# A two-block kernel's expert layer: 64 tokens' first product by gathered rows, dense product at 320 columns, gathers and one-hots placed anew

## The chip, the core and the metric

The kernel runs on one core of a Trainium2 chip. The time is the device time of one execution in microseconds. The engines are TensorE (PE, matmuls; PEld its weight loads), VectorE (DVE), ScalarE (ACT), GpSimd (POOL) and SyncE (SP, which only issues transfers).

## The reference, cut to what matters

The program is two transformer blocks on 512 tokens of width 1024. The change lies in the last layer of the second block, a layer of 16,384 experts (128 x 128), of which each token uses 8 x 16 = 128. Heads and halves choose the experts, the gates are a softmax over 16 scores, and each chosen expert is one row of `expert_u` and one row of `expert_v`.

```python
q = (xb @ w_query).reshape(T, 8, 2, 128)
s = einsum('thpk,hpnk->thpn', q, sub_keys)
top_s, top_i = top_k(s, 16)
cand_s = top_s[:, :, 0, :, None] + top_s[:, :, 1, None, :]
cand_i = top_i[:, :, 0, :, None] * 128 + top_i[:, :, 1, None, :]
best_s, best_pos = top_k(cand_s.reshape(T, 8, 256), 16)
idx = take_along_axis(cand_i..., best_pos)
gate = softmax(best_s)
act = gelu(einsum('td,thkd->thk', xb, expert_u[idx]))
out = einsum('thk,thkd->td', gate * act, expert_v[idx])
```

## The kernel before, in words

The tokens are four tiles of 128. Tile 0 takes the literal way: for each of its 128 choices a **gather**, an indirect DMA that POOL issues (line L1074), brings one row of u, later of v, per token into one of four row buffers (`grow`), and DVE makes one pass over the 128 x 1024 buffer: a product with the tokens' rows `h2`, summed to one number per token (L1077), or an addition of the v row times its weight to `acc0` (L1079). That makes 256 gathers. They are all in `experts_out`.

Tiles 1 to 3 (384 tokens) take the dense way. For each of 128 units j (128 experts each) the **u product** `expert_in` (L1056) multiplies the unit's u weights with all 384 tokens: a weight of 128 x 1024 is loaded, ACT makes its high part (L201), POOL or DVE the rest by a subtraction (L202), and TensorE runs 8 x 3 matmuls of 384 columns (L207 to L209); a gelu follows (L1062). The result is multiplied with a dense matrix of gates, which is zero where a token did not choose the expert, and the **v product** (18 matmuls of 512 columns a unit) adds into six PSUM banks.

The layer runs in this order. `route` (L1088) makes the **keys** in 16 steps (a query product of 24 matmuls of 512 columns, key scores, and the best 16 of 128 on DVE), and then the **selection** for the four tiles in turn (8 steps each: 2048 sums of candidates, best 16 of 256 for each head, masked products on POOL at L1136 that pick the indices, softmax). The indices `eid` and gates of tile 0 serve the gathers; those of the others are transposed into `sel`. `gates_dense` (L1171) makes the **one-hots** in 12 groups of 32 tokens: for each four tokens, four rows A (a one-hot of i times the gate) and one broadcast compare B (one-hot of j), and 128 x 128 matmuls of the two give the 16,384 gates of a token. A comes from POOL for two of eight fours (`GP`, L1188), from ACT for two (`GA`, L1192, L1193, with the gate then on DVE's B at L1195) and from DVE for four (L1199); B is L1202; ACT copies the result to `gst` (L1206), and it goes to DRAM (`gD`). `experts_out` (L1214) is the **output**: gates come back from `gD`, and unit by unit the gated u results go through the v product.

A pace table in `peer` (L1024) spreads 64 of the 128 u products (the even units) between the steps of `route` and `gates_dense`, with their subtraction on POOL; their results are spilled to DRAM (`actD`) and read back in the output. The other 64 are made in the output, with the subtraction on DVE, beside the 256 gathers (one to three a unit).

What is written here is not the order on the engines: a planner takes the program with its dependencies and buffers, places each instruction at its engine's next free time by its own table of durations, the earlier in the program first, and so fixes one order for each engine and for each DMA queue. On the chip each engine works through its order strictly, so an instruction that waits holds back all behind it on that engine.

```python
pace = [(1, 3), (15, 10), (32, 37), (24, 14)]
...
for steps, us in pace:
    for i in range(steps):
        _advance(work)
        for _ in range((i + 1) * us // steps - i * us // steps):
            act = self.expert_in(self.gpool or Q, psp, 2 * j, nc.gpsimd, ...)
```

## Time and profile before

| | |
|---|---|
| median of 3 runs | 2302.53 us (2298.85 to 2306.55) |
| the profiled execution's own time | 2311.13 us |
| its span in the profile | 2309.4 us |
| mean granted clock of TensorE | 0.983 of full speed |
| busy over the span: PE, DVE, ACT, POOL | 2211.4, 1645.3, 955.0, 841.4 us |
| moved by DMA | 469.53 MB, 203 GB/s over the span |

A row of a group reads: line, engine, operation, tiles written and read with their shapes, count, then busy time in us and the mean length of one in ns, then the idle time of the engine just before them and what ended it. A row of the timeline begins with the start in us from the span's start and the length in us. Instructions of one engine can overlap a little, so that the mean times the count can be more than the busy time.

### The profile page before, as it was taken

The page shows a single profiled execution, that of the slowest core. Times are in us where ns is not written, and L with a number is a line of the kernel's source. Part 1 is how long each engine was busy: PE and PEld are TensorE (multiplying, and loading weights), DVE is VectorE, ACT ScalarE, POOL GpSimd, SP SyncE. Part 2 cuts the span into 40 slices and gives each one's busy share as a digit, 9 for nine tenths or more (in the row PEclk, how much of TensorE's full clock was granted, in tenths as well). Part 3 has the DMA queues.
Part 4 walks back from the last instruction along what each step waited for, and adds up shares of the span by engine and source line. Part 5 has one row for each costly group of instructions (what it writes and reads, how often), then busy time and mean ns, then how long its engine had stood idle before and what let it go on. Part 6 is the DMA issues. An engine that isn't in the chain of part 4 may idle for free. (4 is left out here: it accounts for less than half of the span.)

```text
span 2309.4 us, 32140 instructions
## 1 busy us (share of the span) xinstructions
PE 2211.4 (96%) x11849; PEld 1959.7 (85%) x11849; DVE 1645.3 (71%) x3065; ACT 955.0 (41%) x1540; POOL 841.4 (36%) x619
## 2 busy tenths in 40 slices
PE   7898999999999999999998899979999999999997
PEld 6687888888888888888898889968888888888886
DVE  4336556878635468556589899768888877888888
ACT  4215444343425533353333489823333333333332
POOL 3133210000002224231458898624444444445445
PEclk9998899999999999999999999989999999999999
DMA  7423104766422321053344456799999999899996
GB/s 245 124 63 96 38 1 157 241 216 221 134 100 77 110 76 53 20 185 105 108 145 141 151 189 229 270 326 348 341 341 342 348 347 345 318 336 342 351 333 218
DMA packets 165646, 469.53 MB, mean 203 GB/s; under 512 B 18801, under 2 KB 62705, under 8 KB 165361
## 3 DMA queue, kind: packets, MB, share of 16 engines
q1 hardware_dynamic: 128624, 333.25, 42.3%
q0 software_dynamic: 36864, 134.23, 15.9%
q8 instruction: 93, 1.52, 0.3%
q14 instruction: 65, 0.52, 0.1%
HBM read 422.31 MB, written 39.85 MB: 200 GB/s over the span
## 5 line engine op out<-in xcount | busy, mean ns | idle before, releaser
L207 PE MATMUL b<-hh,wlo 128*128 128x384 f32 (+2 forms) x1872 | 656.1, 352 | 10.7 <-ACT act L1062 5.5
L208 PE MATMUL b<-hl,whi 128*128 128x384 f32 (+2 forms) x1872 | 654.2, 350 | 3.9 <-DVE hl L289 3.3
L209 PE MATMUL b<-hh,whi 128*128 128x384 f32 (+2 forms) x1872 | 653.3, 350 | 0.0
L201 ACT ACTIVATE whi<-raw 128x1024 fp32r<-128x1024 f32 (+1 forms) x405 | 426.3, 1057 | 388.8 <-PE b L209 164.7
L202 DVE TENSOR_TENSOR wlo<-raw,whi 128x1024 fp32r<-128x1024 f32 (+1 forms) x326 | 396.8, 1226 | 216.5 <-ACT whi L201 211.4
L207 PEld LDWEIGHTS b<-hh,wlo 128*128 128x128 f32 x1872 | 354.3, 190 | 38.8 <-issue 7.5
L208 PEld LDWEIGHTS b<-hl,whi 128*128 128x128 f32 x1872 | 355.1, 190 | 31.0 <-DVE hl L289 3.8
L202 POOL TENSOR_TENSOR wlo<-raw,whi 128x1024 fp32r<-128x1024 f32 x79 | 199.6, 2540 | 494.9 <-ACT whi L201 485.6
L209 PEld LDWEIGHTS b<-hh,whi 128*128 128x128 f32 x1872 | 354.7, 189 | 25.3 <-issue 0.4
L207 PE MATMUL b<-whi,wl 128*128 128x512 f32 x768 | 299.9, 390 | 13.1 <-DVE wl L1250 13.1
L208 PE MATMUL b<-wlo,wh 128*128 128x512 f32 x768 | 300.8, 392 | 0.0
L209 PE MATMUL b<-whi,wh 128*128 128x512 f32 x768 | 300.7, 392 | 0.0
L1074 POOL DMA_INDIRECT grow<-in_p_ur_dram,eid x128 | 170.7, 1334 | 249.7 <-DVE gact L1077 173.1
L1074 POOL DMA_INDIRECT grow<-in_p_v_dram,eid x128 | 175.3, 1370 | 208.4 <-DVE acc L1079 131.2
L1062 ACT ACTIVATE act<-b 128x384 f32<-128x384 f32 x114 | 55.8, 491 | 351.3 <-PE b L209 315.3
L207 PE MATMUL b<-whi,hl 128*128 128x512 f32 (+1 forms) x464 | 181.0, 391 | 4.4 <-DVE hl L255 2.4
L207 PEld LDWEIGHTS b<-whi,wl 128*128 128x128 f32 x768 | 144.8, 189 | 42.3 <-DVE wl L1250 13.5
L209 PE MATMUL b<-whi,hh 128*128 128x512 f32 (+1 forms) x464 | 179.6, 387 | 0.0
L208 PE MATMUL b<-wlo,hh 128*128 128x512 f32 (+1 forms) x464 | 179.6, 387 | 0.0
L209 PEld LDWEIGHTS b<-whi,wh 128*128 128x128 f32 x768 | 144.7, 188 | 30.3
L208 PEld LDWEIGHTS b<-wlo,wh 128*128 128x128 f32 x768 | 144.7, 188 | 29.0
L1079 DVE SCALAR_TENSOR_TENSOR acc<-grow,gact,acc 128x1024 f32<-128x1024 f32 x127 | 162.5, 1280 | 6.9 <-DMA grow<-in_p_v_dram,eid 5.7
(296 smaller groups left out, 3065.5 us busy)
## 6 DMA issues: line engine op xcount, KB each, us to landing
raw<-in_p_u_dram SPq DMA_DIRECT2D x128, 512.0 KB, 4.4
raw<-in_p_v_dram SPq DMA_DIRECT2D x128, 512.0 KB, 6.7
raw<-in_w_adaT_dram SPq DMA_DIRECT2D x48, 512.0 KB, 4.2
gD<-gst SPq DMA_DIRECT2D x48, 512.0 KB, 4.3
gt<-gD SPq DMA_DIRECT2D x16, 1536.0 KB, 13.0
raw<-in_w_up_dram SPq DMA_DIRECT2D x44, 512.0 KB, 4.2
raw<-in_w_t_dram SPq DMA_DIRECT2D x32, 512.0 KB, 3.6
acts<-actD SPq DMA_DIRECT2D x64, 192.0 KB, 5.7
```

Source lines behind the costliest of these rows:

```text
L201: nc.scalar.activation(hi, raw, AF.Copy)
L202: (eng or nc.vector).tensor_tensor(lo, raw, hi.bitcast(F32), op=ALU.subtract)
L207: mm(out, al, bh, start=start, stop=False)
L208: mm(out, ah, bl, start=False, stop=False)
L209: mm(out, ah, bh, start=False, stop=stop)
L1062: self.nc.scalar.activation(act, ps, AF.Gelu)
L1074: nc.gpsimd.indirect_dma_start(out=g, out_offset=None, in_=rows[n], in_offset=bass.IndirectOffsetOnAxis(ap=self.eid[:, s:s + 1], axis=0))
L1079: nc.vector.scalar_tensor_tensor(self.acc0, g, act[:, s:s + 1], self.acc0, op0=ALU.mult, op1=ALU.add)
```

## The change

64 of tile 1's tokens leave the dense u product. Tokens 0 to 63 of tile 1 have their 128 choices gathered as 64 gathers of 128 rows (64 tokens, two choices at a time: the upper half of the partitions holds choices 64 to 127, with copies of the indices `eid1` and of the tokens' rows `h2b`). DVE makes one pass over each, and the gelu of the 128 numbers times the gate takes the gate's place in `sel`, so that the activation comes in with the gates; the u results of these 64 tokens are set to 1.0 in the output. Their v product stays dense. The dense u product has 320 columns.

96 of the 128 u products are now made before the output and 32 (every fourth unit) in it. The selection's order is tile 1, 0, 2, 3. The gathers of tile 1 are spread over the selection from tile 0's steps on; 22 of tile 0's gathers lie in the selection, 48 in the one-hots and 187 steps in the output. POOL makes the rows A for four of eight fours instead of two, ACT for two (both steps on ACT, the gate included), DVE for two; for the two groups of 32 tokens that hold tile 1's 64, ACT's two go to DVE, and these groups come last. In the one-hots the u products' subtraction is on DVE instead of POOL. The one-hot matmuls write PSUM with a stride of four elements, and ACT's copy writes runs of four. The pool of split weights is opened anew for the second mixer (8 buffers) and for this layer (6 instead of 8).

```diff
-NSPILL = 64
+NSPILL = 96
+NIN = 320
...
-GP, GA = (2, 6), (0, 4)
+GP, GA = (0, 2, 4, 6), (1, 5)
...
+NACT = 6
...
             if n == 2:
+                wsp.close()
                 late = ctx.enter_context(tc.tile_pool(name="late", bufs=1, reuse_waits="tile"))
                 self.h2 = late.tile([128, D], F32, name="h2")
+            if n > 1:
+                wsp.close()
+                wsp = ctx.enter_context(ExitStack())
+                self.wsp = wsp.enter_context(tc.tile_pool(name=f"wsp{n}", bufs=8 if n == 2 else 6, reuse_waits="tile"))
...
-                                rows=None if tt else self.h2)
+                                rows={0: self.h2, 1: self.h2b}.get(tt))
+            nc.sync.dma_start(self.h2b[64:128], self.h2b[0:64])
...
-                pace = [(1, 3), (15, 10), (32, 37), (24, 14)]
...
+                pace = [(1, 3, 0, 0), (15, 12, 0, 0), (8, 10, 0, 0), (8, 14, 24, 0), (16, 29, 40, 22), (24, 28, 0, 48)]
+                self.pend = []
+                work = [self.route(Q, psp, sel, iota), self.gates_dense(psp, sel, iota)]
+                g1 = [self.gather1(Q, psp, sel)]
+                todo, self.gpool = list(self.slot), None
+                for steps, cols, r1, r0 in pace:
                     for i in range(steps):
+                        part = lambda k: (i + 1) * k // steps - i * k // steps
                         _advance(work)
...
+                        for _ in range(part(cols)):
+                            act = (self.gpool or Q).tile([128, NIN], F32, name="act", bufs=4)
+                            j = todo.pop(0)
+                            self.expert_in(act, psp, j, nc.vector if self.gpool else nc.gpsimd)
+                            nc.sync.dma_start(self.actD[self.slot[j]], act)
+                        _advance(g1, part(r1))
+                        _advance(g0, part(r0))
...
+        ps = psp.tile([128, S], F32, name="u")[:, :NIN]
+        self.proj_t(ps, w, self.hh, self.hl, slice(S - NIN, S))
         self.nc.scalar.activation(act, ps, AF.Gelu)
...
+    def row(self, n, eid):
+        g = self.grows.tile([128, D], F32, name="grow")
+        self.nc.gpsimd.indirect_dma_start(out=g, out_offset=None, in_=self.a[n].rearrange("j i d -> (j i) d"),
+                                          in_offset=bass.IndirectOffsetOnAxis(ap=eid, axis=0))
+        return g
...
+    def gather1(self, Q, psp, sel):
+
+        nc = self.nc
+        act = Q.tile([128, 64], F32, name="gact1")
+        for k in range(64):
+            g = self.row("p_ur", self.eid1[:, k:k + 1])
+            nc.vector.tensor_tensor_reduce(g, g, self.h2b, 1.0, 0.0, ALU.mult, ALU.add, act[:, k:k + 1])
+            if k < 63:
+                yield
+        both = Q.tile([64, 128], F32, name="gact2")
+        nc.scalar.activation(act, act, AF.Gelu)
+        nc.sync.dma_start(both[:, 0:64], act[0:64])
+        nc.sync.dma_start(both[:, 64:128], act[64:128])
+        nc.vector.tensor_tensor(both, both, self.gate1, op=ALU.mult)
+        ps = psp.tile([128, NT, 128], F32, name="t")
+        nc.tensor.transpose(ps[:, 0, :64], both, self.ident[:64, :64])
+        nc.scalar.activation(sel[2][:, 0, :64], ps[:, 0, :64], AF.Copy)
...
-            for t in range(NT):
+            for t in (1, 0, 2, 3):
...
-            for c in range(12):
+            for c in list(range(2, 12)) + [0, 1]:
...
-                    if t4 in GP:
-                        for i in range(4):
-                            nc.gpsimd.tensor_scalar(A[:, i], iota, ii[:, i:i + 1], gg[:, i:i + 1], op0=ALU.is_equal,
-                                                    op1=ALU.mult)
-                    elif t4 in GA:
+                    if t4 in GA and c > 1:
+
                         for i in range(4):
                             nc.scalar.activation(A[:, i], iota, AF.Abs, bias=ii[:, i:i + 1], scale=-1.0)
-                        nc.scalar.activation(A, A, AF.Relu, bias=self.ones, scale=-1.0)
                         for i in range(4):
-                            nc.vector.tensor_scalar(B[:, i], iota, jj[:, i:i + 1], gg[:, i:i + 1], op0=ALU.is_equal,
-                                                    op1=ALU.mult)
+                            nc.scalar.activation(A[:, i], A[:, i], AF.Relu, bias=gg[:, i:i + 1], scale=ng[:, i:i + 1])
                     else:
+                        eng = nc.gpsimd if t4 in GP else nc.vector
                         for i in range(4):
...
+                            eng.tensor_scalar(A[:, i], iota, ii[:, i:i + 1], gg[:, i:i + 1], op0=ALU.is_equal,
+                                              op1=ALU.mult)
...
                     for i in range(4):
-                        nc.tensor.matmul(ps[:, i, :], A[:, i, :], B[:, i, :], start=True, stop=True)
-                    nc.scalar.activation(st.rearrange("p j t -> p t j")[:, 4 * t4:4 * t4 + 4, :], ps, AF.Copy)
+                        nc.tensor.matmul(ps.rearrange("p (j t) -> p t j", t=4)[:, i, :], A[:, i, :], B[:, i, :],
+                                         start=True, stop=True)
+                    nc.scalar.activation(st[:, :, 4 * t4:4 * t4 + 4], ps.rearrange("p (j t) -> p j t", t=4), AF.Copy)
...
+            acts = [P.tile([128, n], F32, name=f"acts{i}") for i in range(NACT)]
+            for t in acts:
+                nc.gpsimd.memset(t[:, :n - NIN], 1.0)
```

## Rows read from the trace of the kernel before

**Rows 1.** Busy time of each engine by stretch; the first line names the columns.

```profile
core 0: us, PE busy (x) PEld busy (x) DVE busy (x) ACT busy (x) POOL busy (x), PEclk, DMA share, GB/s
989.00:1173.00 184.00, 179.73 (x948) 162.91 (x949) 99.71 (x505) 67.42 (x98) 56.26 (x26) 0.99 0.40 133
1173.00:1337.00 164.00, 148.28 (x837) 146.58 (x837) 153.58 (x352) 62.75 (x88) 126.21 (x42) 0.96 0.49 148
1337.00:1490.00 153.00, 146.44 (x1107) 144.31 (x1106) 142.56 (x367) 147.94 (x246) 127.08 (x106) 1.00 0.61 227
1490.00:1514.00 24.00, 11.75 (x67) 11.11 (x65) 7.37 (x10) 6.25 (x12) 1.87 (x2) 0.89 1.01 364
1514.00:2285.00 771.00, 767.32 (x3696) 676.41 (x3697) 630.59 (x819) 272.01 (x376) 339.21 (x250) 0.99 0.93 337
```

**Rows 2.** Timeline of TensorE: start, us, line, tiles; ten or eleven matmuls apart.

```profile
39.83 0.28 PE L207 MATMUL b<-hh,wlo 128*128 128x256 f32 x1
...
41.15 0.28 PE L209 MATMUL b<-hh,whi 128*128 128x256 f32 x1
...
998.49 0.33 PE L208 MATMUL b<-hl,whi 128*128 128x384 f32 x1
...
1000.23 0.33 PE L209 MATMUL b<-hh,whi 128*128 128x384 f32 x1
```

**Rows 3.** Groups of TensorE: one of 989 to 1173, one of 1173 to 1490.

```profile
L207 PE MATMUL b<-hh,wlo 128*128 128x384 f32 x142 | 48.2, 340 | 1.5 <-ACT hh L288 0.9 <-POOL wlo L202 0.6
...
L1205 PE MATMUL b<-gb,ga 128*128 128x128 f32 x768 | 97.0, 276 | 6.6 <-ACT gst L1206 3.9 <-POOL ga L1188 2.4 <-DVE gb L1195 0.4
```

**Rows 4.** Groups of POOL: the first of 989 to 1173, three of 1173 to 1490.

```profile
L202 POOL TENSOR_TENSOR wlo<-raw,whi 128x1024 fp32r<-128x1024 f32 x24 | 57.6, 2412 | 127.6 <-ACT whi L201 118.3 <-issue 5.6 <-PE b L207 3.7
...
L1188 POOL TENSOR_SCALAR ga<-c_iota,sel,sel 128x128 f32<-128x128 f32 x96 | 109.7, 1153 | 21.7 <-PE b L1205 9.7 <-ACT ga L1192 6.7 <-DMA actD<-ga 3.3
L202 POOL TENSOR_TENSOR wlo<-raw,whi 128x1024 fp32r<-128x1024 f32 x40 | 104.1, 2618 | 23.0 <-ACT whi L201 23.0
L1136 POOL TENSOR_TENSOR eq<-eq,fi 128x2048 f32<-128x2048 f32 x8 | 37.1, 4632 | 15.4 <-DVE eq L1134 15.4
```

**Rows 5.** Line L1188 in the one-hots: ns min/median/max of one.

```profile
L1188 POOL TENSOR_SCALAR ga<-c_iota,sel,sel x96: 784/966/2250, 1340.1 to 1482.6; 128x128 f32<-128x128 f32 x96
```

**Rows 6.** Timeline of POOL: the first and third of three gathers.

```profile
1487.66 0.94 POOL L1074 DMA_INDIRECT grow<-in_p_ur_dram,eid  x1 [2.79 <-PE b L1205]
...
1490.15 0.94 POOL L1074 DMA_INDIRECT grow<-in_p_ur_dram,eid  x1 [0.31 <-issue]
```

**Rows 7.** Group of POOL in the output: busy, mean ns.

```profile
L1074 POOL DMA_INDIRECT grow<-in_p_v_dram,eid x127 | 173.5, 1366 | 206.6 <-DVE acc L1079 129.5 <-DVE gact L1077 63.1 <-issue 6.9
```

**Rows 8.** Groups of DVE: two of the one-hots, two of the output.

```profile
L1199 DVE TENSOR_SCALAR ga<-c_iota,sel,sel 128x128 f32<-128x128 f32 x192 | 63.6, 404 | 1.6 <-DMA actD<-ga 0.9 <-PE b L1205 0.5
...
L1202 DVE TENSOR_TENSOR gb<-c_iota,sel 128x512 f32<-128x512 f32 x72 | 48.4, 692 | 0.0
...
L202 DVE TENSOR_TENSOR wlo<-raw,whi 128x1024 fp32r<-128x1024 f32 x181 | 218.4, 1220 | 24.5 <-ACT whi L201 24.2
...
L1077 DVE CUSTOM_DVE_ANT_0 grow<-grow,h 128x1024 f32<-128x1024 f32 x127 | 153.1, 1219 | 4.5 <-DMA grow<-in_p_ur_dram,eid 4.3
```

**Rows 9.** Group of ACT in the one-hots.

```profile
L1206 ACT ACTIVATE gst<-b 128x512 f32<-128x512 f32 x96 | 105.0, 1187 | 4.6 <-PE b L1205 4.4
```

**Rows 10.** Timeline of DVE and of POOL in the selection.

```profile
1228.21 5.93 DVE L1111 TENSOR_TENSOR cand<-val 128x2048 f32<-128x2048 f32 x1
...
1227.38 4.61 POOL L1136 TENSOR_TENSOR eq<-eq,fi 128x2048 f32<-128x2048 f32 x1 [2.47 <-DVE eq L1134]
...
1231.93 4.41 POOL L202 TENSOR_TENSOR wlo<-raw,whi 128x1024 fp32r<-128x1024 f32 x1
```

**Rows 11.** Waits of POOL in the output: us, times, longest.

```profile
POOL grow L1074 <- DVE gact L1077: 225.8, 102, 12.5
```

More of the change, by code (lines that the diff above doesn't have):

```diff
@@ L1025, in peer @@
         tc, nc, a = self.tc, self.nc, self.a
-        dt = slice(128, S)
         n = S - 128
@@ L1035, in peer @@
             self.gate0 = P.tile([128, 128], F32, name="gate0")
+            self.eid1 = P.tile([128, 64], I32, name="eid1")
+            self.grows = c0.enter_context(tc.tile_pool(name="grows", bufs=GROWS, reuse_waits="tile"))
+            g0 = [self.gather(P)]
+            fresh = [j for j in range(128) if (j + 1) * (128 - NSPILL) // 128 > j * (128 - NSPILL) // 128]
+            self.slot = {j: k for k, j in enumerate(j for j in range(128) if j not in fresh)}
             with ExitStack() as c1:
@@ L1038, in peer @@
                 psp = _Banks(self.psum, t=[6, 7], u=[4, 5, 0], g=[1, 2, 3])
-                sel = [Q.tile([128, NT - 1, 128], F32, name=f"sel{i}") for i in range(3)]
+                sel = [Q.tile([128, NT - 1, 128], F32, name=f"sel{i}") for i in range(4)]
+                self.gate1 = Q.tile([64, 128], F32, name="gate1")
                 iota = self.const(Q, "iota")
-                pace = [(1, 3), (15, 10), (32, 37), (24, 14)]
-                work = [self.route(psp, sel, iota), self.gates_dense(psp, sel, iota)]
@@ L1052, in peer, with expert_in @@
+                        _advance(g1, part(r1))
+                        _advance(g0, part(r0))
+                assert not todo
+                _advance(g1, 99)
                 while work:
                     _advance(work)
-            self.experts_out()
-    def expert_in(self, pool, psp, j, eng, tag="act"):
-        n = S - 128
+            self.experts_out(fresh, g0, sum(p[3] for p in pace))
+    def expert_in(self, act, psp, j, eng):
         w = self.unit(self.a["p_u"][j], eng=eng)
-        ps = psp.tile([128, S], F32, name="u")[:, :n]
-        self.proj_t(ps, w, self.hh, self.hl, slice(128, S))
-        act = pool.tile([128, S], F32, name=tag, bufs=6)[:, :n] if tag == "ga" else pool.tile([128, n], F32, name=tag, bufs=4)
+        ps = psp.tile([128, S], F32, name="u")[:, :NIN]
+        self.proj_t(ps, w, self.hh, self.hl, slice(S - NIN, S))
@@ L1072, in gather @@
                 for s in range(16 * h, 16 * h + 16):
-                    g = P.tile([128, D], F32, name="grow", bufs=GROWS)
-                    nc.gpsimd.indirect_dma_start(out=g, out_offset=None, in_=rows[n],
-                                                 in_offset=bass.IndirectOffsetOnAxis(ap=self.eid[:, s:s + 1], axis=0))
+                    g = self.row(n, self.eid[:, s:s + 1])
                     if n == "p_ur":
@@ L1212, in gates_dense, with experts_out @@
             self.gpool = None
-    def experts_out(self):
+    def experts_out(self, fresh, gather, done):
         tc, nc, a = self.tc, self.nc, self.a
@@ L1226, in experts_out @@
             g2 = self.gate_row(P, psp.only("u"), 40, "g2")
-            early = {j: self.expert_in(T, psp.only("pre"), j, nc.vector) for j in (1, 3, 5)}
+            acts = [P.tile([128, n], F32, name=f"acts{i}") for i in range(NACT)]
+            for t in acts:
+                nc.gpsimd.memset(t[:, :n - NIN], 1.0)
+            free = list(range(NACT))
+            early = {}
+            for j in fresh[:3]:
+                early[j] = acts[free.pop(0)]
+                self.expert_in(early[j][:, n - NIN:], psp.only("pre"), j, nc.vector)
             acc = [[psp.tile([128, 512], F32, name="acc") for h in range(2)] for t in range(NT - 1)]
@@ L1236, in parts @@
                                       self.gD[:, :, 256 * g:256 * g + 256].rearrange("c i n -> i c n"))
[L1237 to L1243 removed]
+                if j in early:
+                    act = early[j]
+                else:
+                    act = acts[free[0]]
+                    if j in self.slot:
+                        nc.sync.dma_start(act[:, n - NIN:], self.actD[self.slot[j]])
+                    else:
+                        self.expert_in(act[:, n - NIN:], psp, j, nc.vector)
+                    free.append(free.pop(0))
+                if j in early:
+                    free.append(acts.index(early.pop(j)))
                 v = self.unit(a["p_v"][j])
[L1245 removed]
+                ag = T.tile([128, n], F32, name="ag", bufs=3)
+                nc.vector.tensor_tensor(ag.rearrange("p (c t) -> p c t", t=32), act.rearrange("p (c t) -> p c t", t=32),
                                         gts[g][:, :, jj, :], op=ALU.mult)
@@ L1272, in experts_out @@
             fw = self.rows(P, a["fnorm"], name="fw")
-            done = 0
+            rest, done = 257 - done, 0
             ready = [parts(j) for j in range(AHEAD)]
```

89 lines of the change are left out of this document (45 added, 44 removed).

## The prediction

> **What bounds the kernel now.** I read the table by stretches first [rows 1]. Up to 989 us nothing that matters is touched. From there the table has five stretches: the keys (184 us, the queries and key scores), the selection (164 us), the one-hots (153 us), a gap of 24 us while the first gates come back, and the output (771 us). In the keys and in the output TensorE is busy almost without a break (179.7 of 184, 767.3 of 771). In the selection no engine stands alone: DVE 153.6, TensorE 148.3, POOL 126.2 of 164. In the one-hots ACT 147.9, TensorE 146.4, DVE 142.6 and POOL 127.1 of 153. So the planner packs these stages tightly, and each engine is near its end: the longest engine of selection and one-hots together, DVE with 296 us, stands against 317 us of time. Work that is taken from TensorE there counts only as far as no other engine gets longer than TensorE was.
>
> Then I read the pitch of the matmuls, start to start, because the busy time of one overlaps the next [rows 2]: 256 columns eleven in 1.32 us (0.120), 384 columns ten in 1.74 us (0.174).
>
> **The change, part by part.** *Columns.* 320 lies half-way between 256 and 384, so I take (0.120 + 0.174) / 2 = 0.147 us; the ends are 0.120 and 0.174. One expert's u product is 24 matmuls: 4.18 us before, 3.53 after.
>
> *Output.* The kernel before makes 64 u products after the one-hots, the new one 32. TensorE loses 32 x 4.18 = 134 us and 32 x (4.18 - 3.53) = 21 us more on those that stay, 154 us in all. TensorE sets this stage, so all of it comes off if DVE and the transfers follow. DVE loses 32 subtractions of a u weight at 1.22 us and 66 gather passes at 1.22 [rows 8]: 630.6 - 39 - 81 = 511 us in 617, 83% as before (82%). Transfers: 795 us (gap and output) at 337 GB/s are 268 MB; gone are 32 weights and 66 gathers of 0.524 MB (128 rows of 4 KB) and the spill grows by 96 x 0.164 - 64 x 0.197 = 3.1 MB, which leaves 219 MB in 641 us, 342 GB/s; the gap ran at 364 [rows 1]. I take the 154 us. After: 795 - 154 = 641.
>
> *Keys.* TensorE ran 142 matmuls of 384 columns there on the line shown and as many on its two sister lines, 426 / 24 = 17.7 products [rows 3]; the new program puts 15 before the selection. 184 - 17.7 x 4.18 + 15 x 3.53 = 163 us.
>
> *Selection and one-hots.* Here the change piles up. 81 products of 3.53 us (286 us) and the one-hot matmuls (97 us busy, [rows 3]) give TensorE 383 us. DVE keeps its 153.6 us of selection and gets 86 gather passes (64 for tile 1, 22 for tile 0) at 1.22: 259 us. In the one-hots it makes 96 broadcast compares (48.4 / 72 = 0.67 each, 64 us) and 104 one-hot rows (63.6 / 192 = 0.33, 34 us), 28 subtractions (34 us) and 48 gather passes (59 us): 191 us [rows 8]. Together 450.
>
> POOL gets most. Its subtractions: 68 products leave theirs on POOL; before, POOL had done 24 by the end of the keys, 6 ahead of TensorE with eight weight buffers; with six I take 4 ahead, 19 done, and 49 x 2.41 = 118 us remain. The masked index products stay (8, 37 us) [rows 4]. One-hot rows double from 96 to 192. The instruction alone takes 0.784 at least, 0.966 in the median and 1.153 in the mean [rows 4, 5]; the long ones are those that ran beside DVE's one-hot rows, and these fall from 288 to 104, so I take the median, 185 us (ends 150 and 221). Gathers: 134 move in (86 to the selection, 48 to the one-hots). Three in a row started 1.24 us apart, 0.94 of it the instruction [rows 6], and I take 1.24: 166 us; ends 0.94 (126) and, from the output stage's mean of 1.37 with the same 0.30 us gap, 1.67 (224) [rows 7]. Sum: 118 + 37 + 185 + 166 = 507 us. **POOL is longer than DVE (450) and TensorE (383)**: it was not the longest in any stage before. The idle POOL time in the keys can't take the gathers, whose indices come out of the selection, nor the one-hots.
>
> So keys to one-hots take 163 + 507 = 670 us against 501: 169 us more.
>
> *The rest.* ACT's copy of the gates to SBUF (96 of 1.19 us, [rows 9]) now writes runs of four elements. Whether it gains from that or costs twice as much, ACT's 211 us of the two stages [rows 1] with 105 more stay far from POOL's sum. The strided PSUM writes of the one-hot matmuls have no row; up to double, 97 us more, TensorE has 480 us and still stays under POOL, so I price them at nothing. The reordering of the tiles, the two-half copies of indices, acts and h2 by DMA, the reopened weight pools: a few transfers of 2 us beside other work, and some ten short TensorE and ACT instructions at the end of the second mixer: +1 us, ends 0 and 5. DMAs that wait for gather results sit in SP's queue ahead of weight loads; they are covered as long as POOL is what TensorE waits for.
>
> *Sum:* +169 - 154 + 1 = +16 us. The profiled execution's own time is 2311.1 us (span 2309.4), so 2327 for it; it lies 8.6 us over the median of 2302.5, and against the median the forecast is **2318 us**.
>
> **The rivals.** *DVE paces instead (faster).* If POOL's new work goes at the cheap ends (0.784 and 0.94), its sum is 118 + 37 + 150 + 126 = 431, under DVE's 450, and the stage takes 163 + 450 = 613: 112 - 154 + 1 = -41, 2262 us. The point from which it decides is one number: POOL's sum of 491 makes the change neutral. For it: fewer of DVE's one-hot rows stretch POOL's, and the gap after a gather may lie beside the next instruction's start. Against it: DVE is as full as before, with longer instructions.
>
> *POOL and DVE shut each other out (slower still).* A candidate sum on DVE took 5.93 us, beginning under POOL's 4.61 us product, and the POOL subtraction that began under it took 4.41, where its mean in the keys is 2.41 [rows 4, 10]. All 134 gather passes and 28 subtractions on DVE are of such two-tensor kind, 162 x 1.22 = 198 us; if POOL stands still for a third of them, 66 us, the time is 2384; for all of them it is 2516, which one-hot rows near 0.8 us beside a busy DVE speak against. The Trainium skill, page "SBUF — State Buffer", section "SBUF: two separate sides", says that a DVE instruction with two SBUF inputs and a GpSimd instruction that reads SBUF exclude each other for the whole instruction. By that rule the full 198 us would be lost; the trace agrees for the long POOL instructions and not for the short one-hot rows.
>
> *Waiting for row buffers.* POOL waited 225.8 us in 102 times for DVE to free a gather's buffer in the output [rows 11], 2.2 us each, with nothing queued behind. Now subtractions and one-hot rows are queued behind a gather, and TensorE waits for those. I count it inside the forecast's own range: 30 such waits, fewer than one gather in four, cost 66 us if none overlaps.
>
> *The output gives less.* If transfers hold at the old mean of 337 GB/s, 219 MB take 650 us, 9 more: 2327. If 320 columns cost as much as 384, the output loses 21 us: 2339, and the stages under POOL hide the rest.
>
> **How the numbers follow.** About 0.3% (7 us) is what a measurement of this kernel can tell from no change. The forecast, POOL paces: 0.54, own range 2285 to 2355 (one-hot rows at either end are -35 and +36), of which 0.33 is slower, 0.11 the same, 0.10 faster. DVE paces: 0.26, of which 0.25 faster and 0.01 the same. Shut out: 0.12, slower. The output gives less: 0.08, of which 0.06 slower, 0.01 the same, 0.01 faster. Together faster 0.36, same 0.13, slower 0.51. The range goes from under the DVE case to the shut-out case at a third, 2250 to 2390; a TensorE-paced stage below it, or the full lock above, is left out.
>
> **What would show it.** In the changed profile the stretch from keys to one-hots should be near 670 us with POOL busy nearly all of its last 500, TensorE near 75% there and its clock at times at the lower level, as in the gap before (0.89 [rows 1]); one-hot rows on POOL near 0.97 us, gathers near 1.24 apart; the output near 641 us with TensorE without a break. The forecast is wrong if POOL has idle time while DVE has none (then 2262), if POOL's one-hot rows and subtractions are over 1.2 and 3 us (then 2384), or if TensorE's 320-column pitch is not near 0.147.

## The result and the profile after

The changed kernel takes 2497.4 us in the median (2492.2 to 2499.2, four runs) against 2301.7 for the kernel before (2298.9 to 2306.6, four runs): a ratio of 1.084, 95% interval 1.082 to 1.087. The forecast was 2318 us, its range ended at 2390. The direction held, the size did not. The profiled execution took 2499.2 us, its span is 2497.4; the execution before had 2311.1 and 2309.4, so 188 us have to be found.

The table by stretches of the changed kernel (columns as in [rows 1]: busy time of PE, PEld, DVE, ACT and POOL with instruction counts, granted clock, DMA share, GB/s); keys, selection, three parts of the one-hots, the gap, the output:

```profile
989.00:1165.00 176.00, 174.83 (x992) 158.70 (x993) 99.47 (x504) 67.87 (x101) 58.02 (x27) 0.98 0.41 140
1165.00:1394.00 229.00, 169.11 (x1019) 165.47 (x1018) 228.92 (x404) 71.95 (x112) 177.57 (x75) 0.87 0.54 182
1394.00:1560.00 166.00, 138.12 (x877) 131.45 (x875) 100.49 (x161) 81.25 (x170) 160.36 (x117) 0.90 0.69 244
1560.00:1700.00 140.00, 97.16 (x639) 90.66 (x638) 86.22 (x143) 65.72 (x141) 126.97 (x102) 0.86 0.69 250
1700.00:1777.00 77.00, 38.85 (x161) 31.81 (x162) 48.08 (x78) 10.97 (x19) 65.96 (x55) 0.63 0.56 187
1777.00:1800.00 23.00, 2.77 (x17) 2.51 (x16) 8.62 (x13) 3.01 (x6) 7.31 (x14) 0.65 1.03 409
1800.00:2473.00 673.00, 639.42 (x3000) 541.26 (x3000) 555.56 (x738) 225.07 (x315) 298.36 (x210) 0.98 0.93 339
```

Beside [rows 1] this reads: keys 176 us (184 before, 163 forecast), selection and one-hots 229 + 383 = 612 (317 before, 507 forecast), gap and output 696 (795 before, 641 forecast), the tail behind the last row 24 as before. That is -8, +295, -99 and 0: the 188 us. Against the forecast's own terms it is 13, 105 and 55 us too much. In the selection VectorE has no idle time at all (228.9 of 229). In the one-hots GpSimd is busy 353 of 383 and TensorE 274. The forecast's own term for the two stages, GpSimd's sum of 507 us, was nearly met: GpSimd is busy 531 us there. The other 81 us it stands idle, 51 of them in the selection.

GpSimd's groups in the one-hots, to be held against [rows 4]:

```profile
L1260 POOL TENSOR_SCALAR ga<-c_iota,sel,sel 128x128 f32<-128x128 f32 x192 | 254.0, 1329 | 1.6
L1090 POOL DMA_INDIRECT grow<-in_p_ur_dram,eid x59 | 67.6, 1145 | 15.2 <-issue 10.1 <-DVE gact L1120 3.5 <-DVE gb L1262 0.6
L1090 POOL DMA_INDIRECT grow<-in_p_v_dram,eid x16 | 19.9, 1244 | 12.9 <-DVE acc L1108 3.5 <-DVE gact L1120 2.8 <-DVE acc L1105 1.8
L204 POOL TENSOR_TENSOR wlo<-raw,whi 128x1024 fp32r<-128x1024 f32 x6 | 14.2, 2360 | 0.1
```

A one-hot row takes 1.33 us in the mean, 254 us for 192 of them, where the forecast had 0.966 and 185. There are also 75 gathers in this stretch, not 48: the planner had left only 28 of the 86 in the selection, and 217 of tile 0's 256 behind the one-hots, so that 103 gathers came into the two stages, not 134. VectorE's passes for tile 1 by stretch, the selection first and then the one-hots:

```profile
L1120 DVE CUSTOM_DVE_ANT_0 grow<-grow,h2b 128x1024 f32<-128x1024 f32 x24 | 72.3, 3036 | 0.0
...
L1120 DVE CUSTOM_DVE_ANT_0 grow<-grow,h2b 128x1024 f32<-128x1024 f32 x40 | 50.4, 1266 | 21.6 <-DMA grow<-in_p_ur_dram,eid 21.5
```

The same instruction takes 3.04 us beside GpSimd's long two-input products and subtractions, and 1.27 beside its short rows. Forecast: 1.22 for all.

TensorE's waits from the selection to the one-hots' end, and in the output (line waited for, us in total, times, longest; `gact` are the gathered activations, `wl` the low part of the gated u results):

```profile
PE b L1265 <- POOL ga L1260: 56.0, 52, 2.8
PE b L1129 <- DVE gact L1127: 40.9, 1, 40.9
PE b L209 <- POOL wlo L204: 30.5, 11, 7.5
...
PE b L209 <- DVE wl L1322: 48.0, 11, 24.3
```

The 40.9 us is new: the last two groups of one-hots need tile 1's gathered activations, whose last pass ended at 1712 us. During the wait, 1680 to 1721, GpSimd made no one-hot row; it issued 20 gathers, at least 11 of them tile 0's, and was busy 24 of the 41 us. Behind the wait TensorE waits for GpSimd's rows again, and from 1700 on the granted clock is 0.63 in the mean, between the two levels (1.2 and 2.4 GHz).

### The profile page after: what moved, and what is told of

The parts are those of the page before. It is cut to its first block, busy times and chain, and to the rows that moved or that the text cites. A ratio compares the mean times of both kernels' runs of the same rounds, so it can differ in the third digit from the quotient of the medians.

```text
span 2497.4 us, 32709 instructions
## 1 busy us (share of the span) xinstructions
PE 2201.3 (88%) x11858; PEld 1926.6 (77%) x11858; DVE 1729.9 (69%) x3041; ACT 924.8 (37%) x1587; POOL 1084.3 (43%) x789
## 4 chain that ended last, share of the span: by engine, by line
PE 57%; DVE 14%; POOL 14%; issue 8%; DMA 5%; ACT 2%; SPq 0%; POOLq 0%; DVEq 0%; ACTq 0%
PE b L209 17%; PE b L210 17%; PE b L211 17%; POOL ga L1260 8%; POOL grow L1090 3%; DVE grow L1120 2%; DMA grow<-in_p_v_dram,eid 1%; POOL wlo L204 1%; DMA raw<-in_p_v_dram 1%; PE b L667 1%; DMA acts<-actD 1%; DVE eq L1180 1%; DVE wlo L204 1%; PE b L1147 1%; DVE cand L1155 1%
## 5 line engine op out<-in xcount | busy, mean ns | idle before, releaser
L209 PE MATMUL b<-hh,wlo 128*128 128x320 f32 (+2 forms) x1872 | 646.0, 346 | 47.9 <-POOL wlo L204 35.2
L210 PE MATMUL b<-hl,whi 128*128 128x320 f32 (+2 forms) x1872 | 641.0, 343 | 0.7 <-DVE hl L257 0.6
L211 PE MATMUL b<-hh,whi 128*128 128x320 f32 (+2 forms) x1872 | 639.9, 342 | 0.0
L209 PEld LDWEIGHTS b<-hh,wlo 128*128 128x128 f32 x1872 | 366.1, 196 | 78.0 <-POOL wlo L204 38.5
L210 PEld LDWEIGHTS b<-hl,whi 128*128 128x128 f32 x1872 | 366.6, 196 | 26.5 <-DVE hl L257 1.2
L1090 POOL DMA_INDIRECT grow<-in_p_ur_dram,eid x192 | 243.6, 1269 | 232.6 <-DVE gact L1103 153.9
L204 POOL TENSOR_TENSOR wlo<-raw,whi 128x1024 fp32r<-128x1024 f32 x83 | 214.6, 2592 | 160.3 <-ACT whi L203 160.0
L1260 POOL TENSOR_SCALAR ga<-c_iota,sel,sel 128x128 f32<-128x128 f32 x192 | 254.0, 1329 | 1.6
L209 PEld LDWEIGHTS b<-whi,wl 128*128 128x128 f32 x768 | 147.0, 191 | 83.2 <-DVE wl L1322 53.1
L1265 PE MATMUL b<-gb,ga 128*128 128x128 f32 x768 | 144.6, 325 | 64.3 <-POOL ga L1260 56.0
L1265 PEld LDWEIGHTS b<-gb,ga 128*128 128x128 f32 x768 | 122.4, 224 | 83.5 <-POOL ga L1260 72.7
```

Source lines behind the costliest of these rows:

```text
L204: (eng or nc.vector).tensor_tensor(lo, raw, hi.bitcast(F32), op=ALU.subtract)
L209: mm(out, al, bh, start=start, stop=False)
L210: mm(out, ah, bl, start=False, stop=False)
L211: mm(out, ah, bh, start=False, stop=stop)
L1090: self.nc.gpsimd.indirect_dma_start(out=g, out_offset=None, in_=self.a[n].rearrange("j i d -> (j i) d"), in_offset=bass.IndirectOffsetOnAx ...
L1260: eng.tensor_scalar(A[:, i], iota, ii[:, i:i + 1], gg[:, i:i + 1], op0=ALU.is_equal, op1=ALU.mult)
```

## Experiments

Selection and one-hots are counted here from the last key score to the last one-hot matmul: 609 us in the changed kernel, 313 in the one before.

### The exclusion measured by itself

A small kernel without the model: 40 one-hot rows, 16 subtractions or 32 gathers on GpSimd, alone and beside one kind of VectorE instruction at a time.

```diff
+for what, dve in ((rows, None), (rows, ("tt", 40)), (rows, ("ts", 40)), (rows, ("ttr", 40)), (rows, ("stt", 40)),
+                  (rows, ("ttp", 40)), (rows, ("ttrp", 40)), (rows, ("b", 60)), (wlo, None), (wlo, ("tt", 40)),
+                  (gath, None), (gath, ("tt", 40)),
...
```

> Leaves out the whole model: it only puts GpSimd work beside VectorE work, phase by phase, and writes x back. Theory 'exclusion' (a VectorE instruction with two SBUF inputs and a GpSimd instruction that reads SBUF run one after the other): 40 one-hot rows alone take 40 x 0.79 = 32 us; beside 40 two-input VectorE instructions of 1.22 us (product, pass, scaled sum) the two take turns and rows and VectorE together end after about 32 + 49 = 80 us; beside the one-input form and beside the forms whose second input is in PSUM the rows stay at 0.79 each and the phase ends with VectorE (about 49 us); the subtraction on GpSimd, 2.41 alone, likewise adds (16 x 2.41 + 49 = 88 us); a gather's issue, which reads only its indices, stays near 1.1 us. Rival 'GpSimd is slow beside any busy VectorE' (traffic or a shared share): rows take 1.0 to 1.3 us in all these phases, the phase is as long as the longer engine (50 us), and one input or PSUM makes no difference.

Its groups by instruction, one window for each phase (names: `s` is in SBUF, `hp` in PSUM): rows alone; beside a two-input subtraction; beside a multiplication by a scalar; beside the gather pass; beside the scaled sum (the addition of a v row times its weight); beside the pass with PSUM; beside the broadcast compare; the subtraction on both engines; gathers alone; gathers beside the subtraction.

```profile
L77 POOL TENSOR_SCALAR row<-iota,sc 128x128 f32<-128x128 f32 x34 | 26.4, 797 | 0.0
...
L77 POOL TENSOR_SCALAR row<-iota,sc 128x128 f32<-128x128 f32 x11 | 36.6, 3341 | 0.1
L99 DVE TENSOR_TENSOR do<-s,s 128x1024 f32<-128x1024 f32 x31 | 36.2, 1242 | 0.0
...
L77 POOL TENSOR_SCALAR row<-iota,sc 128x128 f32<-128x128 f32 x14 | 27.8, 2001 | 0.1
L103 DVE TENSOR_SCALAR do<-s,s 128x1024 f32<-128x1024 f32 x40 | 27.4, 761 | 0.0
...
L77 POOL TENSOR_SCALAR row<-iota,sc 128x128 f32<-128x128 f32 x11 | 36.8, 3361 | 0.1
L108 DVE CUSTOM_DVE_ANT_0 do<-s,s 128x1024 f32<-128x1024 f32 x31 | 36.4, 1241 | 0.0
...
L77 POOL TENSOR_SCALAR row<-iota,sc 128x128 f32<-128x128 f32 x16 | 38.2, 2402 | 0.1
L105 DVE SCALAR_TENSOR_TENSOR do<-s,s 128x1024 f32<-128x1024 f32 x31 | 37.7, 1292 | 0.0
...
L108 DVE CUSTOM_DVE_ANT_0 do<-s,hp 128x1024 f32<-128x1024 f32 x21 | 24.1, 1215 | 0.0
L77 POOL TENSOR_SCALAR row<-iota,sc 128x128 f32<-128x128 f32 x30 | 23.3, 792 | 0.0
...
L77 POOL TENSOR_SCALAR row<-iota,sc 128x128 f32<-128x128 f32 x12 | 20.7, 1733 | 0.1
L111 DVE TENSOR_TENSOR do<-iota,s 128x512 f32<-128x512 f32 x31 | 19.8, 713 | 0.0
...
L99 DVE TENSOR_TENSOR do<-s,s 128x1024 f32<-128x1024 f32 x18 | 54.8, 3118 | 0.0
L83 POOL TENSOR_TENSOR wlo<-g,g 128x1024 fp32r<-128x1024 f32 x16 | 52.5, 3318 | 0.0
...
L90 POOL DMA_INDIRECT grow<-in_p_ur_dram,eid x30 | 28.2, 941 | 9.0 <-issue 9.0
...
L99 DVE TENSOR_TENSOR do<-s,s 128x1024 f32<-128x1024 f32 x40 | 45.5, 1211 | 0.0
L90 POOL DMA_INDIRECT grow<-in_p_ur_dram,eid x20 | 38.8, 1939 | 6.2 <-issue 6.2
```

Exclusion holds, but not as equal turns. Beside back-to-back passes VectorE keeps its speed (1.24 against 1.21 us) and GpSimd gets one row through for about three of them: 11 rows in 36 us, a quarter of its own pace. Beside the scaled sum it is one for two (2.40 us). With the second input in PSUM the row is back at 0.79. Three points were expected otherwise. The phase of rows beside the two-input form took 70 us, not 80, but VectorE stood still for 23 us of it while 30 rows ran alone, so its length does not test the sum; the rows above are from the 36 us in which both worked. The scalar multiplication of 1024 columns, with one input, holds GpSimd too (2.00 us a row). And a gather is held as well, 1.94 instead of 0.94. The Trainium skill, page "SBUF — State Buffer", section "SBUF: two separate sides", gives the exclusion for VectorE's two-port modes and for two SBUF inputs against a reading GpSimd instruction; the rows agree on what is held. That the scalar multiplication is of the first kind would fit its 0.76 us for 1024 columns, against 1.21 of the two-input subtraction; no run shows it directly.

The same in the changed kernel: a least-squares fit over its 192 one-hot rows gives 0.74 us plus 0.78 us for each us of overlap with a pass or weight subtraction, 0.60 for each us of a broadcast compare and 0.06 for each us of VectorE's own one-hot rows (it explains 96% of the variance). The two-input instructions overlap them for 105 us and the compares for 50. Without a fit: the 60 rows that met neither took 0.79 us in the mean, the 57 that met only a compare 1.00, the 75 that met a pass or weight subtraction 2.01.

### Passes with one input

```diff
-nc.vector.tensor_tensor_reduce(g, g, self.h2b, 1.0, 0.0, ALU.mult, ALU.add, act[:, k:k + 1])
+for _ in range(2):
+    nc.vector.tensor_scalar(g, g, 1.0, None, op0=ALU.mult)
+nc.vector.tensor_copy(act[:, k:k + 1], g[:, 0:1])
...
```

> The changed kernel with each gather pass of u replaced by two VectorE instructions with one SBUF input (same buffer, same 1024 columns, about the same VectorE time) and a copy of one column; this leaves out the sums over the gathered u rows, of tile 1 and of tile 0, so the gathered acts are not computed. Theory 'exclusion': GpSimd's one-hot rows, 1.33 us in the mean and 255 us in all, fall to about 0.95 and 185 us, because only the broadcast compares and the weight subtractions still exclude them; the one-hots (383 us) shorten by 60 to 70 us, the selection (218 us, where the passes took 3.1 us each against GpSimd's long products) by 30 to 50; the whole near 2390 us (2360 to 2430). Rival 'load' (GpSimd's rows are long because VectorE and the transfers are busy): rows stay at 1.2 us or more and the time stays within 20 us of 2497. Rival 'order' (the loss is that the gathers of tile 1 end late): rows change little, the wait of TensorE for the gathered acts (41 us) stays, time above 2450.

2531.8 us in its one run; selection and one-hots took 613 us, near the changed kernel's 609, GpSimd's rows 1.24 us, and TensorE's wait for the gathered activations was 53.1. It looks like a case for "load" or "order", but the small kernel shows that it tested nothing: the replacement is itself of the kind that shuts GpSimd out. It is inconclusive.

### The second input in PSUM

Two PSUM banks are taken from the u products and the one-hots. The control does that alone; the run fills them with the tokens' rows.

```diff
-psp = _Banks(self.psum, t=[6, 7], u=[4, 5, 0], g=[1, 2, 3])
+psp = _Banks(self.psum, t=[6, 7], u=[4, 5], g=[1, 2], h=[0, 3])
...
-nc.vector.tensor_tensor_reduce(g, g, self.h2b, 1.0, 0.0, ALU.mult, ALU.add, act[:, k:k + 1])
+for i in range(2):
+    c = slice(512 * i, 512 * i + 512)
+    nc.vector.tensor_tensor_reduce(g[:, c], g[:, c], self.hp[i], 1.0, 0.0, ALU.mult, ALU.add, half[:, i, k:k + 1])
```

> The changed kernel with two PSUM banks instead of three for the u products and two for the one-hots before the output: the control for the next run, which needs the two banks. Both theories: within 20 us of 2497, if anything slower (2490 to 2520).

> The changed kernel with the tokens' rows for tile 1's gather passes kept in the two PSUM banks that the control leaves free, so that each pass (now two halves of 512 columns, added up at the end) has one input in SBUF and one in PSUM; nothing is left out. Theory 'exclusion': the 24 passes of the selection, 3.0 us each now, fall to 1.4 (about 35 us of VectorE time there) and the 40 in the one-hots stop holding GpSimd (40 x 1.2 x 0.75 = 36 us); against the control 70 us less (40 to 90), near 2430. GpSimd's one-hot rows fall from 1.33 to about 1.15 us. Rival 'load': the passes cost a little more time than before, rows stay at 1.3, within 15 us of the control or slower.

Control 2496.3 us, with PSUM 2452.9: 43 less, inside the expectation at its lower end. Groups of the control, selection and one-hots:

```profile
L1260 POOL TENSOR_SCALAR ga<-c_iota,sel,sel 128x128 f32<-128x128 f32 x192 | 248.1, 1298 | 1.6
...
L1120 DVE CUSTOM_DVE_ANT_0 grow<-grow,h2b 128x1024 f32<-128x1024 f32 x64 | 123.5, 1946 | 22.0 <-DMA grow<-in_p_ur_dram,eid 21.9
```

The same of the run with PSUM:

```profile
L1267 POOL TENSOR_SCALAR ga<-c_iota,sel,sel 128x128 f32<-128x128 f32 x192 | 221.8, 1161 | 1.7
...
L1126 DVE CUSTOM_DVE_ANT_0 grow<-grow,b 128x512 f32<-128x512 f32 x128 | 81.9, 680 | 30.2 <-DMA grow<-in_p_ur_dram,eid 30.1
```

The same sums over the same rows cost VectorE 42 us less and GpSimd's rows 26 us less; selection and one-hots fall from 606 to 556 us. In the selection the 24 passes fell from 3.04 us to 1.35 (two halves of 0.68), and the stage from 227 to 203 us. This settles that the exclusion, not mere load, lengthened them: no work was taken from either engine. Its size is shown only for tile 1's passes; about 9 of the 50 us are TensorE's long wait for tile 1's last passes, 35 us in the control and 26 here.

### Fewer rows on GpSimd

```diff
-GP, GA = (0, 2, 4, 6), (1, 5)
+GP, GA = (2, 6), (1, 5)
```

> The changed kernel with GpSimd making rows for two of eight fours instead of four; VectorE makes the other two. Theory 'exclusion, GpSimd paces the one-hots': GpSimd loses 96 rows x 1.33 = 128 us, VectorE (about 235 of 383 busy) gains 96 x 0.42 = 40 us; the one-hots fall from 383 to about 275 us and the whole to about 2390 us (2365 to 2420). Rival 'order' (the late gathers of tile 1 set the end of the one-hots): under 40 us gained, above 2455. Rival 'VectorE paces': no gain or slower, 2490 to 2540.

2415.2 us, 82 less than the changed kernel, as "GpSimd paces" had it; the one-hots took 298 us. With PSUM as well, and then with no rows on GpSimd (`GP, GA = (), (0, 1, 4, 5)`):

> The changed kernel with both cures: the second input of tile 1's passes in PSUM, and GpSimd with two of eight fours (VectorE takes the others). Theory 'exclusion, GpSimd paces': the two gains, 44 and 82 us, nearly add, less what the fewer rows no longer wait for: 2385 us (2365 to 2410). Rival 'each only uncovers the next limit': no better than the better of the two, 2405 to 2420.

> The same with no one-hot rows on GpSimd at all: ScalarE makes four of eight fours, VectorE four. GpSimd keeps the index products, the subtractions and the gathers. If GpSimd still paced the one-hots at two fours, another 40 to 60 us are gained (2325 to 2350). The theory says that VectorE paces then (192 + 241 us busy in the run with PSUM, 40 more for rows, in a stretch of 490): 2365 to 2400, within 25 us of the run with two fours.

2382.1 and 2367.9 us. The first adds up (2497 - 82 - 43 = 2372, ten more); the second gains only 14. Selection and one-hots of that last run (table by stretches):

```profile
1164.00:1367.00 203.00, 162.67 (x1009) 159.34 (x1008) 192.24 (x455) 74.61 (x118) 160.83 (x72) 0.91 0.61 197
1367.00:1635.00 268.00, 234.63 (x1682) 229.66 (x1681) 245.78 (x560) 205.26 (x484) 120.42 (x79) 0.95 0.90 333
```

VectorE is busy 438 of 471 us: once GpSimd has no rows, it is the next limit, by the passes that were moved here.

### What tile 1's gathers cost and what the columns give

Without tile 1's gathers, once at 384 columns, with the dense product for all, and once at 320:

```diff
-pace = [(1, 3, 0, 0), (15, 12, 0, 0), (8, 10, 0, 0), (8, 14, 24, 0), (16, 29, 40, 22), (24, 28, 0, 48)]
+pace = [(1, 3, 0, 0), (15, 12, 0, 0), (8, 10, 0, 0), (8, 14, 0, 0), (16, 29, 0, 22), (24, 28, 0, 48)]
...
-NIN = 320
+NIN = 384
```

> The changed kernel without its gathers for tile 1: dense u product at 384 columns again, no gathered activations, everything else as changed (96 products early, 70 of tile 0's gathers before the output, GpSimd with four fours, ScalarE with gate, strided PSUM); 3 instead of 4 buffers for the results, for space. Theory 'exclusion': 64 gathers and passes leave; selection loses about 75 us of VectorE time, the one-hots 40 gathers (1.2 each), as much exclusion again and the 41 us wait, some 120 us; TensorE gets 0.65 us more on each product, of which about 22 us show in the output and as much in the keys: 2497 - 75 - 120 + 45 = about 2345 us (2310 to 2390). Rival 'the loss comes from GpSimd's four fours and tile 0's early gathers, not from tile 1': above 2430.

> The changed kernel without tile 1's gathers but still at 320 columns; this leaves out the u product of tile 1's 64 tokens. Against the run with 384 columns and no gathers for tile 1 (2453) it shows what the fewer columns give, against the changed kernel (2497) what the 64 gathers cost. Theory: GpSimd and VectorE pace selection and one-hots, so the 0.65 us a product show only in the output (34 products, 22 us) and the keys (15, 10 us): 2425 us (2410 to 2440), so the gathers cost some 70 and the columns give some 28. Rival 'TensorE still paces them': 2453 - 80 = 2373 (2360 to 2395).

2453.2 and 2410.2 us. The first falls on the side of its rival: the 64 gathers are not the main loss. The second lies at the lower end of its expectation. The gathers cost 2497 - 2410 = 87 us, the columns give 2453 - 2410 = 43 back, so the idea that names the change loses 44 us net. The two figures are rough: the run at 320 columns was measured twice, 11 us apart, and it keeps four result buffers where the run at 384 has three. The other 150 us are in the rest of it.

### The rest: early products and early gathers

Tile 0's gathers not emitted before the output (tile 1's kept):

```diff
-(16, 29, 40, 22), (24, 28, 0, 48)
+(16, 29, 40, 0), (24, 28, 0, 0)
```

> The changed kernel with none of tile 0's gathers before the output (all 256 in it, spread as before), tile 1's kept. Theory 'exclusion': the one-hots lose some 35 gathers (1.2 us each) and the exclusion of their passes (35 x 1.2 x 0.75), together 70 us; the output gets 44 gathers more, 23 MB, which at 340 GB/s is 68 us if transfers pace it and nothing if TensorE does: 2430 to 2495, likeliest 2460. Rival 'order' (tile 1's gathers end late because tile 0's stand among them): the one-hots lose the 41 us wait as well, and the time is under 2430.

2489.5 us, 8 less, at the upper end of the expectation. Selection and one-hots fell by 43 us (609 to 566), and it is the rival's reason that did it: TensorE's 41 us wait for the gathered activations is gone, while GpSimd's rows stay at 1.34 us. So that wait came from tile 0's gathers standing among tile 1's. The time did not follow, since TensorE's end, 2423 us, was followed by 66 us of gathers: the last one was issued at 2459 and the last instruction ended at 2489. The planner had still put 16 of tile 0's gathers before the output.

From the run at 384 columns (2453), step by step: GpSimd at two fours and no gathers emitted before the output; then the row buffers opened only in the output; then 64 instead of 96 early products.

```diff
-GP, GA = (0, 2, 4, 6), (1, 5)
+GP, GA = (2, 6), (1, 5)
-(16, 29, 0, 22), (24, 28, 0, 48)
+(16, 29, 0, 0), (24, 28, 0, 0)
...
     def peer(self):
...
-            self.grows = c0.enter_context(tc.tile_pool(name="grows", bufs=GROWS, reuse_waits="tile"))
...
     def experts_out(self, fresh, gather, done):
...
+            self.grows = c0.enter_context(tc.tile_pool(name="grows", bufs=GROWS, reuse_waits="tile"))
...
-NSPILL = 96
+NSPILL = 64
```

> Of the change only the larger number of early products (96 instead of 64), with 384 columns, no gathers before the output, GpSimd with two fours, ScalarE with gate, strided PSUM. Selection and one-hots get 33 products more, 138 us of TensorE, on an engine that was busy 291 of 313: +132. Theory 'transfers pace the output': its 268 MB shrink only by 33 weights and grow by the spill, to 257 MB, 755 us at 340 GB/s, so only some 50 us come back and the time is 2385 (2355 to 2410). Rival 'TensorE paces the output': the 138 us come back and it is 2290 to 2315.

> The run with early products only, with the row buffers of tile 0's gathers opened in the output, so that none of them can come earlier (in that run the planner had put 81 there all the same). Theory 'moved work must still be paid': selection and one-hots fall from 492 to about 455 us, where TensorE (438 busy) paces them, and the output, with all 256 gathers, grows from 701 to 760 to 800 by its transfers: 2373 - 37 + 60 to 100 = 2395 to 2440, no better than with the early gathers. Rival 'the early gathers are the loss of that run': 2300 to 2335.

> The same with 64 products before the output as in the kernel before. What is left of the change is the order of the tiles, ScalarE's rows with the gate, the strided PSUM, subtractions on VectorE in the one-hots, the reopened weight pool. Expected near the kernel before, 2300 us (2285 to 2325); over 2340 would mean that one of these small parts costs more than was thought.

2377.2, 2406.0 and 2328.1 us. The first came near its number for another reason than expected: the planner had placed 81 of tile 0's gathers before the output all the same, so selection and one-hots grew more (492 us) than either theory said, and the output (701) came out between the 755 us of the one and the 795 - 138 = 657 of the other. The second, inside its expectation, separates them. Its one-hots, its output to TensorE's end, and what follows:

```profile
1403.00:1600.00 197.00, 197.00 (x1412) 196.94 (x1411) 144.79 (x319) 140.28 (x306) 128.46 (x92) 1.00 0.59 219
1600.00:2299.00 699.00, 676.12 (x3120) 578.25 (x3119) 557.54 (x748) 233.85 (x328) 310.43 (x217) 0.99 0.95 344
2299.00:2379.00 80.00, 0.00 (x0) 0.00 (x0) 54.75 (x67) 0.21 (x1) 48.05 (x40) 0.52 0.78 258
```

TensorE is done at 2299 us and the last gathers at 2379. While TensorE works some 31 gathers get through in 100 us, with the transfers at 344 GB/s, and in the kernel before it was 32; all 256 took 779 us here. So the output before (795 us) was bound twice, by TensorE and nearly as tightly by its gathers, and 32 u products fewer in it buy nothing unless gathers leave too. That transfers and not the four row buffers hold the gathers to this pace is argued from the DMA share of 0.95; no run separates the two. The third run, with what is left of the change, is 0.9% over the kernel before (1.0059 to 1.0117), 28 us over what was expected as likeliest and just over its range; 18 us of it lie in selection and one-hots, and which small part costs them was not tried.

### Two looks for a gain

The strided PSUM write alone, in the kernel before, and 320 columns with 64 early products, PSUM and more rows on ScalarE:

```diff
-nc.tensor.matmul(ps[:, i, :], A[:, i, :], B[:, i, :], start=True, stop=True)
+nc.tensor.matmul(ps.rearrange("p (j t) -> p t j", t=4)[:, i, :], A[:, i, :], B[:, i, :],
+                 start=True, stop=True)
...
-GP, GA = (0, 2, 4, 6), (1, 5)
+GP, GA = (2, 6), (0, 1, 4, 5)
-NSPILL = 96
+NSPILL = 64
```

> The kernel before with one part of the change alone: the one-hot matmuls write PSUM with a stride of four elements and ScalarE's copy writes runs of four. The copy falls from 1.19 to 0.60 us (96 of them, 57 us of ScalarE's 141 in the one-hots), the matmuls' pitch stays at 0.11. Both theories: TensorE is busy 140 of the one-hots' 146 us, so the time stays within 0.3% of the kernel before (2296 to 2309); a gain of over 10 us would mean that ScalarE paced the one-hots.

> A candidate to beat both kernels: 320 columns and tile 1's gathers with the second input in PSUM, but 64 products before the output as in the kernel before, none of tile 0's gathers before it, GpSimd with two fours, ScalarE with four, VectorE with two. Selection and one-hots: VectorE 158 + 64 x 1.36 + 64 (compares) + 55 (rows) = 365 us against 313 before; keys 10 less; output 64 x 0.65 = 42 less if TensorE paces it, 0 if the transfers do: 2302 + 52 - 10 - 42 = 2302 (2285 to 2350), above 2335 if the output gives nothing.

The first: 2298.9 us, ratio 0.9983 (0.9966 to 1.0), no change that can be told; ScalarE's copy fell as expected, and TensorE is busy 138 of the one-hots' 142 us:

```profile
L1207 ACT ACTIVATE gst<-b 128x512 f32<-128x512 f32 x96 | 56.0, 592 | 30.5 <-PE b L1205 29.7
```

The second: 2430.1 us, a miss by 128 and far outside its range. Its planner put 42 of tile 0's gathers early, VectorE was busy 403 of 449 us in selection and one-hots, and the output gave nothing:

```profile
1615.00:2417.00 802.00, 757.92 (x3818) 661.26 (x3816) 608.99 (x786) 280.41 (x399) 323.69 (x231) 0.97 0.86 310
```

No version here beats the kernel before by more than can be measured.

## Why the prediction was wrong

**Columns.** Right: 0.146 us a matmul against the forecast's 0.147. Timeline of TensorE in the keys, the first and the tenth of a row of 320-column matmuls:

```profile
1100.19 0.30 PE L209 MATMUL b<-hh,wlo 128*128 128x320 f32 x1
...
1101.50 0.31 PE L209 MATMUL b<-hh,wlo 128*128 128x320 f32 x1
```

**Keys.** 176 instead of 163. TensorE is full there (174.8 of 176), and 155 matmuls of one line are 19 products, not 15: work that was moved, not lost.

**Selection and one-hots: the step that failed.** "POOL gets most ... 507 us" took one-hot rows at 0.966 us, passes at 1.22 on VectorE and gathers at 1.24, each from rows in which the other engine did something else, and then took the longer engine's sum. In fact rows cost 1.33 (+69 us), the selection's passes 3.04 (+43 us on VectorE), and the selection was VectorE's (229 us, forecast 262 on GpSimd), while the planner had put 27 gathers more than forecast into the one-hots (383 us, forecast 245). For GpSimd, which loses against passes, what counts is its own sum and some 0.8 of the passes that overlap it.

The reading behind 0.966 was wrong in the kernel before already: "the long ones are those that ran beside DVE's one-hot rows". Of its 96 rows the 19 that met no compare, pass or subtraction took 0.86 us in the mean, the 66 that met only compares 1.19, the 11 that met a pass or subtraction 1.44. Timeline of the kernel before, a row beside VectorE's own rows, one beside two compares, one beside a subtraction:

```profile
1358.60 0.84 POOL L1188 TENSOR_SCALAR ga<-c_iota,sel,sel 128x128 f32<-128x128 f32 x1
1358.26 0.90 DVE L1195 TENSOR_SCALAR gb<-c_iota,sel,sel 128x128 f32<-128x128 f32 x3
...
1360.24 1.78 POOL L1188 TENSOR_SCALAR ga<-c_iota,sel,sel 128x128 f32<-128x128 f32 x1
1360.16 1.28 DVE L1202 TENSOR_TENSOR gb<-c_iota,sel 128x512 f32<-128x512 f32 x2
...
1418.63 1.92 POOL L1188 TENSOR_SCALAR ga<-c_iota,sel,sel 128x128 f32<-128x128 f32 x1
1418.83 1.21 DVE L202 TENSOR_TENSOR wlo<-raw,whi 128x1024 fp32r<-128x1024 f32 x1
```

So the short rows did not speak against the exclusion: "one-hot rows near 0.8 us beside a busy DVE" were those beside VectorE's own short rows, which hold GpSimd hardly at all, and hardly a gather pass ran beside a one-hot row (two gathers came before the output). The rival "shut each other out" named the mechanism, with 2516 us for the full price and 2384 for a third. The time came out at 2497, but that this is near 2516 is partly luck: the stage missed by 105 us, about half of that rival's 198, and the output's 55 come on top.

Rows and passes over their price (69 and 43 us) and the wait of the next paragraph (41) make more than the stage's 105; 31 gathers that did not come (31 x 1.24 = 38 us) go off it. The parts overlap, so this shows their size and not an exact bill. Of the signs that were set for being wrong, rows over 1.2 us were met (1.33), subtractions over 3 us were not (2.66 in the selection, 2.36 in the one-hots). GpSimd also had idle time while VectorE had none, in the selection, which the forecast took for the sign of the faster case; here VectorE was full because its passes took 3.04 us. The count of VectorE's one-hot rows was off too, 112 and not 104, some 3 us. The rule of the Trainium skill that the forecast named, page "SBUF — State Buffer", section "SBUF: two separate sides", is borne out in kind, with GpSimd the loser beside passes (3.34 us a row) and both engines beside long subtractions (3.12 and 3.32).

**What is late next** was not named for the gathered activations: they enter by a gate that the last two groups need, and TensorE stood 41 us for it. The run without tile 0's early gathers shows this as a cost of its own, beside the exclusion.

**Output.** 696 instead of 641. TensorE's busy time fell from 779 to 642 us (137, forecast 154), and its idle time grew from 16 to 54: 24.3 at the start, where the first gates and spilled results come back (clock 0.65 in the gap), 24 in ten waits for VectorE's `wl`. Of the forecast's 154 us 99 came off, "if DVE and the transfers follow", and with no gathers moved it would have been less: in the run without early gathers (at 384 columns) the last of them end 80 us behind TensorE. What sets the waits for `wl` stays open. The number of gathers does not: in the run at 320 columns without tile 1's gathers 35 fewer were left, TensorE's end came 693 us after the last one-hot matmul as in the changed kernel, and its waits for `wl` were 48 us in both; only what follows TensorE's end fell, from 30 to 9 us.

**The bill, by single steps of the runs** (ratios to the kernel before, each step on top of those ahead of it): the small parts 1.009; 96 early products 1.044; gathers allowed early 1.032; GpSimd at four fours and 70 gathers emitted early 1.066; 320 columns 1.046; tile 1's gathers 1.084. The fourth step is GpSimd's rows nearly alone, since 81 and 82 of tile 0's gathers came before the one-hots' end without and with it.

## What to carry to other kernels

Before moving work between VectorE and GpSimd, or beside them, look which of their instructions hold each other, and price each instruction from a row in which the future neighbour runs, not from the same engine's quiet rows. An operand in PSUM takes a VectorE pass out of the exclusion without removing any work. A result that the next stage waits for should not queue behind gathers that nobody waits for yet. A stage that is full on TensorE may be as full on its gathers, so look which of them would set its end before counting on TensorE's part.

## What the runs showed of the hardware that was not expected

A short GpSimd instruction of 0.79 us beside back-to-back VectorE instructions finishes once in two or three of them: 3.36 us beside passes of 1.24, 2.00 beside multiplications of 0.76, 1.73 beside compares of 0.71, 2.40 beside scaled sums of 1.29. VectorE hardly notices (1.24 against 1.21 us for the two-input subtraction). Beside GpSimd's own two-input subtraction of 1024 columns both slow down (3.12 and 3.32 us against 1.21 and 2.34 alone). A gather's issue doubles beside them, 0.94 to 1.94 us. A PSUM write with a stride of four elements costs the matmul nothing (768 of them were busy for 95.7 us in the kernel before with that part alone, 97.0 without it [rows 3]), and with its contiguous runs ScalarE's copy out takes half the time.
